# Out-projection weights of a hybrid attention block: the row sums and the gated halves moved to other steps

## The chip, the cores and the metric

One Trainium2 chip, one of its cores. The time is the device time of one execution in microseconds; a kernel's time is the median of its runs.

## The reference, cut to what matters

A block over 2048 latent tokens of width 1024, with 256 context tokens ahead of them. In float32:

```
mod   = silu(c) @ w_ada + b_ada                      # shift, scale, gate of 1024 each
h     = rmsnorm(x) * (1 + scale) + shift             # also for the context tokens
proj  = h @ w_in                                     # 1024 x 4096: q k v gate of two head groups
y     = [neighbourhood attention | retention] * silu(gates)
out   = rmsnorm(x + gate * (y @ w_out))
```

The change concerns `gate * (y @ w_out)`. `gate` is one number per output column, so the kernel multiplies the columns of `w_out` by it once, ahead of the projection, and stores the product. For that it needs `gate = silu(c) @ w_gate + b_gate`, where `w_gate` is the last third of `w_ada`.

## The kernel before, in words

The kernel is written in program order: each engine works through its own instructions in the order in which the Python code emits them, and nothing reorders them. TensorE computes all products in float32 halves (a rounded high part and the rest), three matmuls for each product. The order of the work around the change is this.

1. A first pass over the tokens, then a first stretch of values (`values`, with `u_v` and `tokform`, L374).
2. **The first pair of blocks** (`strassen(T, 0, 1, ...)`): the columns for q and the two gates, as a 2 x 2 product with seven multiplications (`w_set`, `prod`, L671). It runs over six sets of 256 columns (`SETS`). Each set has seven products of twelve 512-column matmuls, and four steps: after the 2nd, 4th, 6th and 7th product `step(n)` runs what is due. So a pair has 24 steps, 0 to 23; I number them so. `hooks` is a list of 24 lists of functions, one for each step. `w_sums` prepares the next set's weights one step at a time: casts on ScalarE (L624), subtractions on GpSimd (L625), sums on VectorE (L634 to L642).
3. **The second values** (the second call of `values`): ten units of 48 matmuls (L374), numbered 0 to 9. The stretch begins with the two context units, for which the normalised context is loaded again from DRAM (`cS`, L835). Beside it, `pump` drives the sums `h_sums` for the next pair, from blocks 2 and 3 that are loaded again (`hS`, L826).
4. **The second pair of blocks** (`strassen(T, 2, 3, ...)`), again 24 steps. Then attention, retention and the output.

The out-projection weights come in pieces of 128 x 512, two for each 128 rows, in a tile `wraw` with two buffers: sixteen pieces of `w_gate`, then sixteen of `w_out`.

- `wo_gate` (L744, VectorE) adds one piece of `w_gate`, times silu(c), to a running sum `gacc`. Sixteen calls, at steps 1 to 16 of the first pair.
- `wo_row` (L751 on TensorE, L752 on ScalarE) sums `gacc` over its partitions. One call, at step 19.
- `wo_mul` makes one gated half: it multiplies a piece of `w_out` by the row in place (L756, VectorE), casts it into a tile `g` (L758, ScalarE), subtracts (L759, GpSimd), and defers two stores to DRAM (`woS`, L761, on ScalarE's queue) and the next load of `wraw` (L739, on SyncE's queue). `g` has one buffer. Before, four calls lie beside the second values, after units 2, 4, 6 and 8, and twelve in the second pair, at its steps 0, 2, ... 22.

Stores and loads that are deferred wait in a list; `tick()` counts it down and issues what is due. It runs at the start of each step and at the end of each unit. At step 20 of the first pair `take(3)` issues four reloads of block 3; at step 21 `take_a` issues the two context loads and then four reloads of block 2. All of them are issued by SyncE, which works through its queue in order.

Of the kernel before, what the change touches and what calls it, by code (L numbers as in the profile page):

```python
# [82 lines left out]
def hybrid_kernel(ctx: ExitStack, tc: tile.TileContext, a: dict, out: bass.AP):  # L83
# [54 lines left out]
    def defer(n, fn):  # L138
        later.append([n, fn])

    def tick():
        for e in later:
            e[0] -= 1
        due = [e for e in later if e[0] <= 0]
        later[:] = [e for e in later if e[0] > 0]
        for e in due:
            e[1]()
# [190 lines left out]
    def w_parts(rw, lo=3, n=1):  # L338
        wh = wa.tile([P, KC, WG], F32R, name="whi")
        wl = wa.tile([P, KC, WG], F32R, name="wlo")  # L340

        def part(u, c):
            ks = slice(u * KH + c * KH // n, u * KH + (c + 1) * KH // n)
            h, l, r = wh[:, ks, :], wl[:, ks, :], rw[u][:, c * KH // n:(c + 1) * KH // n, :]
            nc.scalar.copy(h, r)
            eng = nc.gpsimd if lo >> u & 1 else nc.vector
            eng.tensor_tensor(l, r, f(h), ALU.subtract)  # L347

        return (wh, wl), [(lambda u=u, c=c: part(u, c)) for u in range(2) for c in range(n)]

    def w_split(rw, lo=3):
        w, parts = w_parts(rw, lo)
        for p in parts:
            p()
        return w
# [52 lines left out]
    def u_v(w, c0, tp):  # L408
        pm = yield from tokform(w, tp)
        vt = op.tile([P, 4, 4, 64], F32R, name="o")  # L410
        pv = pm.rearrange("p (g e d) -> p g e d", e=2, d=64)
        nc.scalar.copy(vt[:, :, ::3, :], pv)
        nc.vector.tensor_tensor(vt[:, :, 1:3, :], pv, f(vt)[:, :, ::3, :], ALU.subtract)
        s, o = (c0 - 1024) // WG, f(vt).rearrange("p (t h) e d -> p t (h e d)", t=2)
        if tp == 8:
            store(vS[s].rearrange("(t p) h d -> p t (h d)", p=P), o)
            return
        for e, j in enumerate(VORD):
            k0, cw = CWIN[j]
            dst = vB[s][:4 * cw, tp, e, :].rearrange("(t r c) d -> r c t d", t=2, r=2)  # L420
            for r in range(2):
                defer(1 + r, lambda dst=dst[r], src=o[64 * r + k0:64 * r + k0 + cw]: nc.sync.dma_start(dst, src))
# [62 lines left out]
    wcur = []  # L485
# [128 lines left out]
    def w_sums(rw):  # L614
        cut2 = lambda t: t.rearrange("p k w -> p (k w)").rearrange("p (s h k c) -> p s h k c", s=2, h=2, k=KH)
        a11, a21 = rw[0][:, :, 0:P], rw[0][:, :, P:WG]
        a12, a22 = rw[1][:, :, 0:P], rw[1][:, :, P:WG]
        W, tl = {}, {}

        def cut(key, n, s, r):  # L620
            if n not in tl:
                tl[n] = cut2(wa.tile([P, KC, WG], F32R, name=("whi", "wlo")[n % 2]))
            t = W[key] = tl[n][:, s]
            nc.scalar.copy(t[:, 0], r)  # L624
            nc.gpsimd.tensor_tensor(t[:, 1], r, f(t)[:, 0], ALU.subtract)  # L625

        V = nc.vector.tensor_tensor

        def p0():
            cut("a11", 0, 0, a11)  # L630
            cut("a12", 0, 1, a12)

        def p1():
            V(a11, a11, a21, ALU.subtract)  # L634
            V(a12, a12, a22, ALU.subtract)
            V(a12, a12, a11, ALU.add)
            V(a21, a21, a22, ALU.add)
            cut("a22", 1, 1, a22)

        def p2():  # L640
            cut("s4", 1, 0, a12)
            V(a22, a22, a11, ALU.subtract)  # L642

        def p3():
            cut("s3", 2, 1, a11)
            cut("s2", 2, 0, a22)

        def p4():
            cut("s1", 3, 0, a21)

        return W, [p0, p1, p2, p3, p4, None, load_w]
# [90 lines left out]
    def wo_gate(k, n):  # L742
        t, acc = wo["w"].pop(0), wo["acc"][:, n * 512:(n + 1) * 512]
        nc.vector.scalar_tensor_tensor(acc, t, silc[:, k, 0:1], acc, ALU.mult, ALU.add)  # L744
        defer(1, wo_next)
# [8 lines left out]
    def wo_mul(k, n):  # L754
        t, sl = wo["w"].pop(0), slice(n * 512, (n + 1) * 512)
        nc.vector.tensor_tensor(t, t, wo["acc"][:, sl], ALU.mult)  # L756
        w = wo["p"].tile([P, 2, 512], F32R, name="g")
        nc.scalar.copy(w[:, 0, :], t)  # L758
        nc.gpsimd.tensor_tensor(w[:, 1, :], t, f(w)[:, 0, :], ALU.subtract)  # L759
        for hl in range(2):  # L760
            defer(1, lambda hl=hl: nc.scalar.dma_start(woS[hl][k, :, sl], f(w)[:, hl, :]))  # L761
        defer(1, wo_next)
# [3 lines left out]
    def unit(g):  # L766
        for _ in g:
            pump["y"] += 1
            if pump["q"] and pump["y"] % pump["every"] == 0:
                pump["q"].pop(0)()  # L770
        tick()

    def strassen(T, A, B, W, mine, hook, last):
        for n, c0 in enumerate(SETS):
            if n + 1 < len(SETS):
                Wn, ahead = w_sums(wcur.pop(0))
            else:
                Wn, ahead = last, plain_next(last)
            w_set(c0, W, T, A, B, mine, ahead, hook)
            W, mine = Wn, ahead  # L780

    def values(vu, hook, at):
        for n, (w, c0, tp) in enumerate(vu):
            unit(u_v(w[0], c0, tp))
            if n == at:
                W, mine = w_sums(wcur.pop(0))
            if at <= n < at + 3:
                mine[n - at]()
            for fn in hook.get(n, ()):
                fn()  # L790
        while pump["q"]:
            pump["q"].pop(0)()
        mine[3]()
        return W, mine

    def vunits(order):
        return [(w, c0, tp) for w, c0, b in order for tp in (2 * b, 2 * b + 1) if tp < 9]
# [21 lines left out]
    w1 = w_split(wcur.pop(0), lo=0)  # L819
    load_w()  # L820
    spill_ctx(1)
    W, mine = values(vunits([([w0], 1024, 0), ([w0], 1024, 1), ([w1], 1280, 0), ([w1], 1280, 1)]), {0: [wo_open]}, 4)

    def take(b):
# [14 lines left out]
    hooks = [[] for n in range(24)]  # L839
    for k in range(8):  # L840
        for n in range(2):
            hooks[2 * k + n + 1].append(lambda k=k, n=n: wo_gate(k, n))
    hooks[19].append(wo_row)
    halves = [lambda k=k, n=n: wo_mul(k, n) for k in range(8) for n in range(2)]
    hooks[20].insert(0, lambda: take(3))
    hooks[21].insert(0, take_a)
    hooks[21].append(lambda: raws.pop(0)())
    mid = []
    strassen(T, 0, 1, W, mine, hooks, mid)
    w1 = []  # L850
    pump.update(y=0, every=4, q=raws)
    W, mine = values(vunits([(mid, 1024, 4), (mid, 1024, 3), (w1, 1280, 4), (w1, 1280, 3), (mid, 1024, 2), (w1, 1280, 2)]),
                     {0: [lambda: w1.append(w_split(wcur.pop(0), lo=0)), load_w, load_w], **{n: [halves.pop(0)] for n in (2, 4, 6, 8)}}, 6)
    T = T2
    hooks = [[] for n in range(24)]
    for n in range(12):
        hooks[2 * n].append(halves.pop(0))
    last = []
    strassen(T, 2, 3, W, mine, hooks, last)
# [762 lines left out]
```

## Time and profile before

| | |
|---|---|
| median of 3 runs | 1360.33 us (1356.68, 1360.33, 1361.18) |
| profiled execution, its own time | 1357.68 us |
| its span, first to last instruction | 1355.7 us |
| mean granted TensorE clock | 0.996 |
| TensorE busy | 1310.1 us, 97% of the span |

Times in the profile are microseconds from the start of the span. A row of the timeline is the start, the duration, the engine, the line, the operation, the tiles, the count, and in brackets how long the engine had been idle and what released it. SPq and ACTq are the instruction queues of SyncE and ScalarE, from which transfers are issued. In the order of the first pair, the last set (steps 20 to 23) runs from 332.8 to 352.7, and the second values from 352.7 to 411.5.

### The profile page before, as it was taken

How to read it: one execution, taken by the hardware profiler on the slowest of the kernel's cores; microseconds unless marked ns; L12 is line 12 of the kernel's file. 1: busy time of each engine (PE TensorE's matmuls, PEld its weight loads, DVE VectorE, ACT ScalarE, POOL GpSimd, SP SyncE). 2: the span in 40 equal slices, each digit the busy share in tenths (PEclk: the TensorE clock that was granted, in tenths of full speed). 3: DMA queues.
4: the chain of work that ended last, by engine and by line, in shares of the span. 5: the costliest groups of instructions: out<-in, count | busy, mean ns of one | idle time of the engine just before them, and what ended most of it. 6: DMA issues, size and time to landing. Idle time of an engine off the chain costs nothing.

```text
span 1355.7 us, 23094 instructions
## 1 busy us (share of the span) xinstructions
PE 1310.1 (97%) x8236; PEld 1146.9 (85%) x8236; DVE 828.3 (61%) x1444; ACT 606.5 (45%) x1259; POOL 579.9 (43%) x569
## 2 busy tenths in 40 slices
PE   6999999999999999999999999999999899999997
PEld 2477899887897788998999889889999789888886
DVE  5687366676766755377767777776654633445345
ACT  4454343343533344455555465556643244333432
POOL 4443101554034664445535474655523154544442
PEclk9999999999999999999999999999999999999999
DMA  9386788464867656978587886666528888555433
GB/s 363 135 279 231 259 313 215 164 210 147 326 182 230 216 203 213 265 210 211 148 225 207 226 224 206 195 181 193 163 90 291 278 290 279 159 163 171 163 121 129
DMA packets 172085, 287.25 MB, mean 212 GB/s; under 512 B 17345, under 2 KB 92225, under 8 KB 170690
## 3 DMA queue, kind: packets, MB, share of 16 engines
q1 hardware_dynamic: 139554, 228.35, 55.8%
q10 hardware_dynamic: 32416, 57.42, 11.8%
q8 instruction: 66, 1.08, 0.3%
q14 instruction: 49, 0.40, 0.1%
HBM read 194.48 MB, written 91.23 MB: 211 GB/s over the span
## 4 chain that ended last, share of the span: by engine, by line
PE 70%; DVE 9%; DMA 8%; POOL 4%; issue 4%; ACT 3%; SPq 1%; ACTq 0%; DVEq 0%; POOLq 0%
PE mm L374 17%; PE mm L671 12%; PE mm L1463 11%; PE mm L363 7%; PE sS L1025 4%; PE tr L1052 3%; PE po L1073 3%; PE mm L1187 2%; PE mm L311 2%; PE tr L1054 2%; PE po L1075 2%; DMA v<-rvS 1%; PE mm L1375 1%; POOL hlo L531 1%; PE mm L1374 1%
## 5 line engine op out<-in xcount | busy, mean ns | idle before, releaser
L374 PE MATMUL mm<-whi,hlo 128*128 128x256 f32 x832 | 228.6, 282 | 1.0 <-DMA hlo<-cS 1.0
L374 PE MATMUL mm<-whi,hhi 128*128 128x256 f32 x768 | 224.3, 292 | 0.0
L374 PE MATMUL mm<-wlo,hhi 128*128 128x256 f32 x768 | 216.8, 282 | 0.0
L1056 ACT CAST pt<-tr 128x640 fp32r<-128x640 f32 (+1 forms) x128 | 95.6, 747 | 160.4 <-PE tr L1054 157.8
L1062 DVE TENSOR_TENSOR pt<-tr,pt 128x640 fp32r<-128x640 f32 (+1 forms) x128 | 114.0, 890 | 78.4 <-ACT pt L1056 77.2
L374 PEld LDWEIGHTS mm<-whi,hlo 128*128 128x128 f32 x832 | 156.6, 191 | 1.4 <-DMA hlo<-cS 1.3
L1045 POOL TENSOR_SCALAR sp<-sp,stt 128x640 f32<-128x640 f32 (+2 forms) x128 | 103.1, 808 | 106.3 <-DVE stt L1044 75.7
L374 PEld LDWEIGHTS mm<-whi,hhi 128*128 128x128 f32 x768 | 146.3, 191 | 0.0
L374 PEld LDWEIGHTS mm<-wlo,hhi 128*128 128x128 f32 x768 | 146.1, 190 | 0.0
L1034 DVE CUSTOM_DVE_ANT_0 sp<-sS,nb 128x640 f32<-128x640 f32 (+2 forms) x128 | 105.6, 825 | 33.4 <-DMA nb<-in_rpb_t_dram 20.7
L1039 ACT ACTIVATE sp<-sp,stt 128x640 f32<-128x640 f32 (+2 forms) x128 | 107.4, 839 | 20.3 <-DVE stt L1034 19.1
L625 POOL TENSOR_TENSOR whi<-st,whi 128x512 fp32r<-128x512 f32 x48 | 62.8, 1330 | 107.7 <-ACT whi L624 107.7
L363 PE MATMUL mm<-hhi,whi 128*128 128x512 f32 x256 | 108.2, 423 | 0.0
L363 PE MATMUL mm<-hlo,whi 128*128 128x512 f32 x256 | 102.0, 399 | 6.0 <-DVE hlo L265 2.1
L1025 PE MATMUL sS<-k,q 128*128 128x256 f32 (+3 forms) x512 | 99.1, 315 | 5.1 <-DVE stt L1034 4.7
L363 PE MATMUL mm<-hhi,wlo 128*128 128x512 f32 x256 | 102.0, 398 | 0.3 <-DVE wlo L347 0.3
L671 PE MATMUL mm<-hhi,whi 128*128 128x512 f32 x336 | 98.1, 395 | 1.6 <-POOL whi L625 1.6
L1463 PE MATMUL mm<-wor,y 128*128 128x512 f32 x384 | 95.7, 398 | 1.1 <-DVE xt L1472 1.1
L1472 DVE TENSOR_TENSOR xt<-mm,xt 128x512 f32<-128x512 f32 x64 | 43.9, 687 | 82.6 <-PE mm L1463 82.5
L1025 PEld LDWEIGHTS sS<-k,q 128*128 128x128 f32 x512 | 82.8, 188 | 12.0 <-DVE stt L1034 8.2
L1463 PE MATMUL mm<-won,y 128*128 128x512 f32 x336 | 89.9, 406 | 0.0
L625 POOL TENSOR_TENSOR wlo<-st,wlo 128x512 fp32r<-128x512 f32 x36 | 53.1, 1476 | 75.8 <-ACT wlo L624 73.7
(258 smaller groups left out, 3051.5 us busy)
## 6 DMA issues: line engine op xcount, KB each, us to landing
st<-in_w_in_dram SPq DMA_DIRECT2D x64, 512.0 KB
q<-qS SPq DMA_DIRECT2D x64, 256.0 KB
hlo<-hS SPq DMA_DIRECT2D x20, 512.0 KB
k<-kS SPq DMA_DIRECT2D x16, 576.0 KB
kS<-o SPq DMA_DIRECT2D x16, 512.0 KB
vB<-o SPq DMA_DIRECT2D x64, 128.0 KB
qS<-o ACTq DMA_DIRECT2D x16, 512.0 KB
woS<-g ACTq DMA_DIRECT2D x32, 256.0 KB
```

What stands on the lines that cost most here:

```text
L363: nc.tensor.matmul(pm[:, :n], ww[:, k, cs], h[:, k, :], start=(k == 0 and i == 0), stop=(k == KC - 1 and i == 2))
L374: nc.tensor.matmul(pm[:, t * WG:(t + 1) * WG], h[:, k, o:o + P], ww[:, k, :], start=(k == 0 and i == 0), stop=(k == KC - 1 and i == 2))
L625: nc.gpsimd.tensor_tensor(t[:, 1], r, f(t)[:, 0], ALU.subtract)
L671: nc.tensor.matmul(pm, ww[:, k, :], hh[:, k, :], start=(k == 0 and i == 0), stop=(k == KH - 1 and i == 2))
L1025: nc.tensor.matmul(o, hd["q"][i][:, hl, j * P:(j + 1) * P], k, start=(hl == 0), stop=(hl == 1))
L1034: nc.vector.tensor_tensor_reduce(T["sp"][:, :n], T["s"], nbz[big][:, o:o + n], -1.0, 3e38, ALU.add, ALU.min, T["st"][:, 0:1])
L1039: nc.scalar.activation(sp[:, :n], sp[:, :n], AF.Exp, bias=st[:, 0:1], scale=-1.0, accum_out=st[:, 1:2])
L1045: nc.gpsimd.tensor_scalar(sp[:, :n], sp[:, :n], st[:, 2:3], 0.0, ALU.mult, ALU.add)
L1056: nc.scalar.copy(pt[:, :ng_ + 2, 0, :], tr[:, :ng_ + 2, :])
L1062: nc.vector.tensor_tensor(pt[:, :n, 1, :], tr[:, :n, :], f(pt)[:, :n, 0, :], ALU.subtract)
L1463: nc.tensor.matmul(pm, yy[:, k, :], ww[:, k, sl], start=(k == 0 and i == 0), stop=(k == 3 and i == 2))
L1472: nc.vector.tensor_tensor(xts[t][:, sl], pm, xts[t][:, sl], ALU.add)
```

## The change

The sixteen `wo_gate` calls move to steps 1 to 12 (four of these steps get two). `wo_row` moves from step 19 to step 14. Six gated halves run in the first pair, at steps 16, 17, 18, 19, 22 and 23; none is left beside the second values; ten stay in the second pair, at its steps 0, 2, ... 18, so that steps 20 and 22 have none. At the end of `values`, one `tick()` is added ahead of the last piece of the weight sums.

```diff
@@ values
         while pump["q"]:
             pump["q"].pop(0)()
+        tick()
         mine[3]()
@@ the first pair
     for k in range(8):
         for n in range(2):
-            hooks[2 * k + n + 1].append(lambda k=k, n=n: wo_gate(k, n))
-    hooks[19].append(wo_row)
+            hooks[1 + (2 * k + n) * 3 // 4].append(lambda k=k, n=n: wo_gate(k, n))
+    hooks[14].append(wo_row)
     halves = [lambda k=k, n=n: wo_mul(k, n) for k in range(8) for n in range(2)]
     hooks[20].insert(0, lambda: take(3))
     hooks[21].insert(0, take_a)
     hooks[21].append(lambda: raws.pop(0)())
+    for n in (16, 17, 18, 19, 22, 23):
+        hooks[n].append(halves.pop(0))
@@ the second values
-                     {0: [lambda: w1.append(w_split(wcur.pop(0), lo=0)), load_w, load_w], **{n: [halves.pop(0)] for n in (2, 4, 6, 8)}}, 6)
+                     {0: [lambda: w1.append(w_split(wcur.pop(0), lo=0)), load_w, load_w]}, 6)
@@ the second pair
-    for n in range(12):
+    for n in range(10):
         hooks[2 * n].append(halves.pop(0))
```

ScalarE's order from step 18 to step 20 of the first pair, before. The two L685 are the activations of set 4's last outputs, ggS are their stores, the `whi` casts belong to the next set's weights, and L699 takes the last set's first product:

```order
L624 CAST wlo<-st 128x512
L685 ACTIVATE o_2748<-o_2748 128x512
L685 ACTIVATE o<-o 128x512
L151 DMA ggS_81<-o_2748 128x512
L151 DMA ggS_82<-o 128x512
L624 CAST whi<-st 128x512 x2
L752 COPY gacc<-mm 128x512 x2
L699 COPY e<-mm 128x512
```

And of the changed kernel:

```order
L624 CAST wlo<-st 128x512
L758 CAST g<-wraw 128x512
L685 ACTIVATE o_2766<-o_2766 128x512
L685 ACTIVATE o<-o 128x512
L761 DMA woS_91<-g 128x512
L761 DMA woS_92<-g 128x512
L151 DMA ggS_81<-o_2766 128x512
L151 DMA ggS_82<-o 128x512
L624 CAST whi<-st 128x512 x2
L758 CAST g<-wraw 128x512
L699 COPY e<-mm 128x512
L761 DMA woS_91<-g 128x512
```

The row copies L752 have left this place; two casts of gated halves (steps 18 and 19) and the stores of the halves of steps 18 and 19 now stand among the activations.

SyncE's queue around the reloads of step 20, before. `st` are weight loads; in brackets stands what an issue waits for: an engine, or the completion of an earlier transfer (the DMAHW names are eight completion counters that the transfers of both queues take turns on):

```order
L739 DMA wraw<-in_w_out_dram 128x512 [waits DMAHW4_49,DVE_49]
L176 DMA st<-in_w_in_dram 128x1024 [waits DMAHW2_49,Pool_49]
L176 DMA st<-in_w_in_dram 128x1024 [waits DMAHW7_49,DMAHW3_49,Pool_49]
L826 DMA hlo<-hS_90 128x1024 [waits DMAHW7_49,PE_49]
L826 DMA hlo<-hS_90 128x1024 [waits DMAHW0_49]
L826 DMA hlo<-hS_90 128x1024 [waits DMAHW2_49]
L826 DMA hlo<-hS_90 128x1024 [waits DMAHW3_49]
L835 DMA hlo<-cS_93 128x2048 [waits DMAHW4_49,PE_49]
```

And of the changed kernel (the lines of `take` are L827 and L836 there):

```order
L176 DMA st<-in_w_in_dram 128x1024 [waits DMAHW6_49,DMAHW3_49]
L176 DMA st<-in_w_in_dram 128x1024 [waits DMAHW7_49]
L739 DMA wraw<-in_w_out_dram 128x512 [waits DMAHW3_49,Pool_49]
L739 DMA wraw<-in_w_out_dram 128x512 [waits DMAHW1_49,Pool_49]
L827 DMA hlo<-hS_90 128x1024 [waits DMAHW3_49,PE_49]
L827 DMA hlo<-hS_90 128x1024 [waits DMAHW4_49]
L827 DMA hlo<-hS_90 128x1024 [waits DMAHW6_49]
L827 DMA hlo<-hS_90 128x1024 [waits DMAHW7_49]
L836 DMA hlo<-cS_93 128x2048 [waits DMAHW0_49,PE_49]
```

Two loads of `wraw` that wait for GpSimd now stand directly ahead of the reloads of block 3; the second of them fills the buffer that the half of step 19 frees.

ScalarE's order beside the last units of the second values, before (L412 casts a unit's values, L624 prepares the second pair's first weights):

```order
L412 CAST o<-mm 128x4x2x64
L761 DMA woS_91<-g 128x512
L761 DMA woS_92<-g 128x512
L624 CAST wlo<-st 128x512
L412 CAST o<-mm 128x4x2x64
L624 CAST wlo<-st 128x512
L758 CAST g<-wraw 128x512
L412 CAST o<-mm 128x4x2x64
L761 DMA woS_91<-g 128x512
```

And of the changed kernel:

```order
L624 CAST whi<-st 128x512 x2
L412 CAST o<-mm 128x4x2x64
L624 CAST wlo<-st 128x512
L412 CAST o<-mm 128x4x2x64
L624 CAST wlo<-st 128x512
L412 CAST o<-mm 128x4x2x64
```

The casts and the stores of the gated halves are gone from this stretch, and so are the loads of `wraw` that stood between the stores of values on SyncE's queue.

## Rows read from the trace of the kernel before

**Rows 1.** The page, busy time, share and instructions of each engine.

```profile
PE 1310.1 (97%) x8236; PEld 1146.9 (85%) x8236; DVE 828.3 (61%) x1444; ACT 606.5 (45%) x1259; POOL 579.9 (43%) x569
```

**Rows 2.** TensorE's waits, 190 to 560: total, times, longest.

```profile
PE mm L671 <- POOL whi L625: 1.6, 3, 1.2
PE mm L374 <- DMA hlo<-cS: 1.0, 1, 1.0
PE mm L671 <- ACT wlo L624: 0.7, 1, 0.7
PE mm L671 <- POOL wlo L625: 0.6, 1, 0.6
```

**Rows 3.** Timeline of TensorE: the row sum, the context unit, the last value matmul.

```profile
331.51 1.88 PE L751 MATMUL mm<-gacc,one 128*128 128x512 f32 x4
332.83 0.79 PE L671 MATMUL mm<-hhi,whi 128*128 128x512 f32 x1
...
353.96 0.38 PE L374 MATMUL mm<-whi,hlo 128*128 128x256 f32 x1 [1.02 <-DMA hlo<-cS]
...
411.40 0.28 PE L374 MATMUL mm<-wlo,hhi 128*128 128x256 f32 x1
```

**Rows 4.** Timeline of SyncE's queue, the reloads of block 3 and the context.

```profile
338.68 1.75 SPq L826 DMA_DIRECT2D hlo<-hS  x4
344.43 0.80 SPq L835 DMA_DIRECT2D hlo<-cS  x2
```

**Rows 5.** Stretches: busy time by engine, PEclk, DMA share, GB/s.

```profile
325.00:338.00 13.00, 13.00 (x54) 9.93 (x53) 5.95 (x9) 5.65 (x10) 4.77 (x5) 1.00 0.21 78
...
340.00:354.00 14.00, 12.98 (x58) 10.24 (x56) 9.12 (x8) 6.43 (x7) 0.00 (x0) 1.00 1.00 364
```

**Rows 6.** Waits of SyncE's queue, 200 to 540.

```profile
SPq L739 <- POOL g L759: 71.6, 9, 11.7
...
SPq L826 <- PE mm L671: 18.1, 1, 18.1
...
SPq L739 <- DMA woS<-g: 11.9, 5, 4.7
```

**Rows 7.** Timeline of ScalarE, steps 18 and 19 of the first pair.

```profile
330.35 0.63 ACT L685 ACTIVATE o<-o 128x512 f32<-128x512 f32 x1 [6.40 <-DVE o L710]
...
332.44 1.23 ACT L685 ACTIVATE o<-o 128x512 f32<-128x512 f32 x2 [0.44 <-DVE o L716]
333.10 0.92 ACTq L151 DMA_DIRECT2D ggS<-o  x2
334.12 1.14 ACT L624 CAST whi<-st 128x512 fp32r<-128x512 f32 x2 [0.45 <-ACT o L685]
```

**Rows 8.** Timeline of GpSimd: weights at step 19, a gated half.

```profile
334.82 2.54 POOL L625 TENSOR_TENSOR whi<-st,whi 128x512 fp32r<-128x512 f32 x2 [1.47 <-ACT whi L624]
...
403.78 1.29 POOL L759 TENSOR_TENSOR g<-wraw,g 128x512 fp32r<-128x512 f32 x1
```

**Rows 9.** Timeline of ScalarE beside the second values.

```profile
395.04 0.81 ACTq L761 DMA_DIRECT2D woS<-g  x2
...
418.00 0.59 ACT L412 CAST o<-mm 128x512 fp32r<-128x512 f32 x1 [1.63 <-DMA vB<-o]
418.02 0.88 ACTq L761 DMA_DIRECT2D woS<-g  x2
```

**Rows 10.** Timeline of SyncE's queue beside the second values.

```profile
397.63 0.36 SPq L739 DMA_DIRECT2D wraw<-in_w_out_dram  x1
...
422.85 0.36 SPq L739 DMA_DIRECT2D wraw<-in_w_out_dram  x1
```

**Rows 11.** Stretches near the start, columns as in Rows 5.

```profile
72.00:76.00 4.00, 2.59 (x13) 1.84 (x11) 4.00 (x6) 3.36 (x6) 2.32 (x2) 1.00 0.57 202
76.00:80.00 4.00, 3.45 (x10) 2.76 (x11) 4.00 (x4) 3.09 (x4) 4.00 (x2) 0.66 0.96 256
...
100.00:104.00 4.00, 2.56 (x13) 1.86 (x13) 4.00 (x5) 0.86 (x3) 2.98 (x1) 1.00 0.27 111
```

## The prediction

> **What bounds the kernel now.** I read the page first. TensorE is busy for 97% of the span and no other engine comes near [rows 1], so an edit on the other engines shows only where it makes or ends a wait of TensorE. No matmul is added or removed. I therefore asked for TensorE's waits in the stretch that the change touches, from the middle of the first pair to the start of attention [rows 2]. There are four groups, 3.9 us together. That is the most that the change can win, 0.29% of the time. 1.0 us of it is the first context unit, which waits for the context reload and goes on at 353.96 [rows 3]. The other 2.9 us lie in the second pair, where TensorE waits for the weight casts and subtractions of the next set.
>
> Why those are late is seen in ScalarE's timeline: it casts the last unit of values at 418.00, after a wait for the stores of an earlier unit [rows 9], while TensorE issued that unit's last matmul at 411.40 [rows 3]. ScalarE enters the second pair 6.6 us behind. The stores are late because SyncE's queue, which issues them in order, stood still ahead of them: its loads of `wraw` wait for GpSimd's subtraction, 71.6 us in all, and for the stores of a gated half on ScalarE's queue, 11.9 us [rows 6].
>
> Then I looked at the place where the work goes. There the reloads are issued by SyncE as soon as TensorE lets go of the buffer: block 3 at 338.68, the context at 344.43 [rows 4]; that wait of SyncE for TensorE is the 18.1 us in its list [rows 6]. Ahead of it the transfer engines are nearly idle, share 0.21 from 325 to 338; from 340 to 354 they are full, share 1.00 at 364 GB/s [rows 5]. So the context lands when all the bytes ahead of it have been moved, and TensorE already waits 1.0 us for it.
>
> **The change part by part.**
>
> *Row sums in twelve slots, row sum at step 14.* The same sixteen VectorE operations, four matmuls and two copies, earlier. The four matmuls of `wo_row` take the 1.3 us from 331.51 to 332.83 [rows 3]; moved ahead they delay steps 15 to 19 by 1.3 us and leave step 20 where it was. Two steps lie between the last `wo_gate` and the row sum, where there were three; TensorE shows no wait for it. Cost 0; were that cover gone, TensorE would wait for the last piece, one VectorE operation, below 1 us.
>
> *No halves beside the second values.* Four multiplications, casts and subtractions, eight stores and four loads leave the stretch in which ScalarE falls behind. With no load of `wraw` in SyncE's queue the eight stores of a unit are issued one behind the other, and the next cast need not wait. The 6.6 us of delay should mostly go, and with it the 2.9 us of waits. Bounds: 0, if the sums for the next pair alone keep ScalarE behind, and -2.9. Halves still run in every second step of the second pair, so I keep 0.3 us: **-2.6 us**. Of the two halves that leave steps 20 and 22 there I expect nothing, since TensorE hardly waits there.
>
> *Four halves in four steps running.* This is where I expect the loss. `g` has one buffer, so the cast of a half waits until the stores of the half before have landed; these stores wait for GpSimd, and they stand in ScalarE's queue at the start of the next step. I follow ScalarE from the activation that follows set 4's sixth product, 330.35 before [rows 7], now 331.65. Its end, the two stores of step 17's half (0.81 us, [rows 9]), one ggS store and a weight cast bring it to 334.2. How long such stores take to land is bounded by two rows: issued until 395.85, and the load behind them goes at 397.63, 1.8 us; issued until 418.90 and followed at 422.85, 3.95 us [rows 9, 10]. The transfers are few at this place, so I take 1.8. Step 18's cast then runs at 334.9 and ends at 335.5; the two activations (1.23) end at 336.7, the stores of its half at 337.5, the two ggS stores (0.92) at 338.4, the two weight casts (1.14) at 339.5 [rows 7]. Step 19's cast ends at 340.1. GpSimd has two weight subtractions first (2.54, then 1.29 for the half, [rows 8]): from 339.0 to 341.5, and the half until 342.8.
>
> Now SyncE. Directly ahead of block 3's reloads stands the load of `wraw` that takes the buffer of step 19's half, so it waits until 342.8. The reloads follow at about 343.2 instead of 338.68, **4.5 us later**, and the context behind them. In addition 0.26 MB of this load or of the half's stores has to be moved in the full stretch, 0.7 us at 364 GB/s [rows 5]. TensorE then waits about 6.2 us at the context unit instead of 1.0: **+5.2 us**. Bounds: 0 for the order if ScalarE and GpSimd finish before 338.68, then only bytes remain (0.8 MB, 2.2 us); and 4.3 us more if the stores of steps 17 and 18 each take 3.95 us to land.
>
> The Trainium skill ("DMA: Bandwidth & Descriptors", on issuing engines that are not separate DMA queues) says that transfers of all issuing engines run on the same 16 DMA engines and interleave. If that did not hold, the stores on ScalarE's queue would cost the reloads nothing and the sum would be 0.7 us lower. The full share in [rows 5] agrees with the rule.
>
> *What an idle TensorE costs behind it.* From 72 to 76 TensorE was busy for 2.59 of 4 us, and in the 4 us that follow the granted clock is 0.66 on the mean, a part of it at the lower level of 1.2 GHz; from 100 to 104 it was busy for 2.56 of 4 us without such a fall [rows 11]. A wait of 6 us is longer than either, so I expect the fall: 4 us at 0.66 and some at less than 1 behind it lose about **+1.7 us**. Bounds 0 and, if it comes twice, 3.4. The Trainium skill ("TensorE: Matmul & The Clock Gate", why this matters) warns of idle gaps between matmul bursts, behind which the clock is back at the lower rate; by it the fall is certain, by the row at 100 it is not, and without it the sum is 1.7 lower.
>
> *Halves at steps 22 and 23.* Their loads and stores (0.5 and 1.0 MB) come behind the context reload. ScalarE waits for them ahead of the first unit's cast, but TensorE has six accumulators and a unit takes 5.8 us, so nothing shows; if the second context unit's weights came late too, 1 us.
>
> *The added tick.* It issues four stores of values ahead of two casts that stand on other engines. SyncE's order stays the same: 0.
>
> **Sum.** -2.6 + 5.2 + 1.7 = +4.3 us on the profiled execution's 1357.68, that is 1362.0. That execution lies 2.65 us below the median and 1.7 us below the mean of the three runs (1359.4). Carried over by the mean, the median of the changed kernel should be **1363.7 us**, 3.4 us or 0.25% over the median of before. About 0.3% (4.1 us) is what a measurement of this kernel tells from no change.
>
> **The rivals.**
>
> A, my forecast: the reload waits behind the load of `wraw`. Chance 0.60. Its own range is 1359.5 (no fall of the clock, one store time less) to 1366; the bound of 0.3% lies in its middle, so I give half of it to slower and a little more to the same.
>
> B, the reload is not held: VectorE's product of step 19 is ready soon after 334, and were ScalarE not held at `g`, GpSimd would be through at 338. Then only the bytes remain, +2.2 - 2.6 = -0.4: 1359.0. For it speaks that ScalarE idles between its rows at 330 to 334 [rows 7]; against it the single buffer of `g`. Chance 0.25, the same.
>
> C, slower: the chain of `g` runs at the upper store time. Then GpSimd ends step 19's weight subtractions not at 341.5 but at 345.8, and the fifth product of the last set, which starts when the fourth is done at about 344.4 [rows 4], waits for them, besides a reload that is 4.3 us later still: +8.6, 1368.0. It decides from a store time of about 3.2 us on. Chance 0.10.
>
> D, faster: the waits of the second pair go in full and the reload is no later, -2.9 or at most -3.9 if the context came in time too: 1356.5. That is inside the bound of 0.3%, so only a run to run shift on top would show it as faster. Chance 0.05.
>
> **How the numbers follow.** Slower: 0.32 of A and C, 0.42. Faster: D, 0.05. The same: 0.28 of A and B, 0.53. The range leaves out the lower part of D and the upper of C: 1357.5 to 1368.
>
> **What would show it.** Right: in TensorE's waits the one for hlo<-cS grows to 5 to 7 us; SyncE's first reload of block 3 is issued at 342 to 345 behind a load of `wraw`; ScalarE's waits name woS ahead of L758; the granted clock drops for a few us after 359; the waits of L671 for L624 and L625 in the second pair shrink below 0.6 us. Wrong: the reload still goes at 338.7, or the context wait stays below 3 us, or the second pair's waits stay at 2.9 us, which would mean that the sums for the next pair and not the halves hold ScalarE.

## Result, and the profile after

The changed kernel takes 1362.44 us (median of 20 runs), the kernel before 1358.45 us (20 runs) on the same chips: a ratio of 1.0029, 95% interval 1.0018 to 1.0039. That is 4.0 us more, where 3.4 had been forecast. The profiled execution took 1363.55 us, its span 1361.7, 6.0 us over the span of before; it lies 1.1 us above its median, and that of before 0.8 below.

TensorE's waits from 190 to 570 (total, times, longest), to be held against [rows 2]:

```profile
PE mm L374 <- DMA hlo<-cS: 8.1, 2, 6.2
PE mm L671 <- POOL whi L625: 1.3, 1, 1.3
```

The waits for L624 and L625 in the second pair are gone. The one for the context has grown from 1.0 to 8.1 us, and one for `whi` has come in a new place, the last set of the first pair. TensorE's timeline shows where, beside [rows 3]:

```profile
347.05 1.67 PE L671 MATMUL mm<-hhi,whi 128*128 128x512 f32 x6 [1.33 <-POOL whi L625]
...
361.48 0.55 PE L374 MATMUL mm<-whi,hlo 128*128 128x256 f32 x1 [6.20 <-DMA hlo<-cS]
363.94 0.58 PE L374 MATMUL mm<-whi,hlo 128*128 128x256 f32 x1 [1.91 <-DMA hlo<-cS]
```

SyncE's queue, beside [rows 4]:

```profile
332.93 0.88 SPq L176 DMA_DIRECT2D st<-in_w_in_dram  x2
342.40 6.20 SPq L739 DMA_DIRECT2D wraw<-in_w_out_dram  x2
348.70 2.16 SPq L827 DMA_DIRECT2D hlo<-hS  x4
350.96 1.48 SPq L836 DMA_DIRECT2D hlo<-cS  x2
```

The first row, two weight loads, is needed further down. The issue of two loads of `wraw` lasts until 348.6, and only then do the reloads go: at 348.70 instead of 338.68, 10.0 us later. TensorE has the last piece of the context at 363.94 instead of 353.96, again 10.0 us later. What holds the loads is read on ScalarE and GpSimd, beside [rows 7, 8]. ScalarE, the casts of the halves of steps 17, 18 and 19, and one pair of stores:

```profile
330.43 0.62 ACT L758 CAST g<-wraw 128x512 fp32r<-128x512 f32 x1 [2.51 <-DMA woS<-g]
...
332.61 0.81 ACTq L761 DMA_DIRECT2D woS<-g  x2
...
340.33 0.62 ACT L758 CAST g<-wraw 128x512 fp32r<-128x512 f32 x1 [5.69 <-DMA woS<-g]
...
346.14 0.62 ACT L758 CAST g<-wraw 128x512 fp32r<-128x512 f32 x1 [1.21 <-DMA woS<-g]
```

The stores of step 17's half are issued until 333.42 and the cast that waits for them starts at 340.33: 6.9 us. GpSimd follows the casts:

```profile
341.08 1.29 POOL L759 TENSOR_TENSOR g<-wraw,g 128x512 fp32r<-128x512 f32 x1 [5.07 <-ACT g L758]
...
344.49 2.51 POOL L625 TENSOR_TENSOR whi<-st,whi 128x512 fp32r<-128x512 f32 x2 [2.11 <-ACT whi L624]
346.95 1.30 POOL L759 TENSOR_TENSOR g<-wraw,g 128x512 fp32r<-128x512 f32 x1
```

The weight subtractions end at 347.0, which is TensorE's wait of 1.3 us, and step 19's half at 348.25, which frees the buffer for SyncE's load. The stretches behind the idle time, then the second values from the end of the first pair on and the second pair, with the columns of [rows 5]. Of after:

```profile
359.00:362.00 3.00, 0.52 (x1) 0.28 (x1) 3.00 (x4) 0.29 (x1) 0.00 (x0) 0.72 0.96 407
362.00:365.00 3.00, 1.09 (x6) 1.06 (x6) 2.90 (x4) 0.00 (x0) 0.00 (x0) 0.50 1.00 404
365.00:368.00 3.00, 3.00 (x19) 3.00 (x19) 2.97 (x6) 1.20 (x2) 0.00 (x0) 0.64 1.04 418
...
355.28:422.90 67.62, 59.51 (x481) 59.25 (x482) 47.59 (x49) 26.71 (x35) 6.49 (x5) 0.95 0.78 249
422.90:539.60 116.70, 116.70 (x507) 94.81 (x506) 75.16 (x88) 46.26 (x79) 67.11 (x49) 1.00 0.61 202
```

And of before:

```profile
352.70:411.50 58.80, 57.78 (x481) 57.54 (x480) 42.15 (x45) 23.55 (x31) 12.19 (x6) 1.00 0.75 234
...
411.50:532.70 121.20, 118.24 (x506) 94.34 (x505) 75.07 (x89) 47.90 (x82) 69.54 (x51) 1.00 0.65 215
```

The second values take 8.8 us more: 7.1 of waits and 1.7 us in which the same matmuls are busy longer (59.51 against 57.78), since behind the idle time the granted clock is 0.50 (the level of 1.2 GHz) from 362 to 365 and a part of the time at that level on both sides. The second pair takes 4.5 us less, 116.7 against 121.2.

### The profile page after: what moved, and what is told of

Same layout as the page of the kernel before. It is cut to its first block, busy times and chain, and to the rows that moved or that the text cites. A ratio compares the mean times of both kernels' runs of the same rounds, so it can differ in the third digit from the quotient of the medians.

```text
span 1361.7 us, 23105 instructions
## 1 busy us (share of the span) xinstructions
PE 1310.5 (96%) x8236; PEld 1148.8 (84%) x8236; DVE 835.2 (61%) x1444; ACT 606.5 (45%) x1259; POOL 577.6 (42%) x569
## 4 chain that ended last, share of the span: by engine, by line
PE 76%; DVE 6%; DMA 6%; POOL 4%; ACT 3%; issue 3%; SPq 0%; ACTq 0%; POOLq 0%; DVEq 0%
PE mm L374 20%; PE mm L671 15%; PE mm L1466 11%; PE mm L363 7%; PE sS L1028 5%; PE tr L1055 3%; PE po L1076 3%; PE mm L1190 2%; PE tr L1057 2%; PE mm L311 2%; PE po L1078 2%; DMA v<-rvS 1%; POOL hlo L531 1%; PE mm L1378 1%; PE mm L1377 1%
## 5 line engine op out<-in xcount | busy, mean ns | idle before, releaser
L625 POOL TENSOR_TENSOR whi<-st,whi 128x512 fp32r<-128x512 f32 x48 | 65.2, 1379 | 137.6 <-ACT whi L624 102.0
L1466 PEld LDWEIGHTS mm<-wor,y 128*128 128x128 f32 x384 | 69.9, 188 | 17.3 <-issue 3.4
```

Source lines behind the costliest of these rows:

```text
L1466: nc.tensor.matmul(pm, yy[:, k, :], ww[:, k, sl], start=(k == 0 and i == 0), stop=(k == 3 and i == 2))
```

## The experiments

All ten hang on the same two numbers: how long the first pair and the second values take together (from the first to the last of their matmuls), and how long the second pair takes. The table gives them from the profiled execution of each kernel, as differences of the starts of the first matmuls of the stages, with the time of SyncE's first reload of block 3 (not corrected for when the pair began), and the ratio to the kernel before with its interval.

| kernel | first pair + values | second pair | reload | ratio |
|---|---|---|---|---|
| before | 177.2 | 121.2 | 338.68 | |
| the change | 188.0 | 116.7 | 348.70 | 1.0029 (1.0018 to 1.0039) |
| no halves at 22, 23 | 186.1 | 116.7 | 346.30 | 1.0028 (1.0013 to 1.0042) |
| loads held | 183.7 | 116.7 | 338.60 | 0.9986 (0.9974 to 0.9998) |
| values' halves to the second pair | 176.6 | 122.8 | 339.25 | 1.0039 (1.0026 to 1.0053) |
| sums, row and tick alone | 176.7 | 123.5 | 339.21 | 0.9993 (0.9978 to 1.0008) |
| 16, 18, 22, 23 | 178.7 | 116.7 | 338.49 | 0.9965 (0.9952 to 0.9978) |
| 16, 17, 18, 22, 23 | 184.1 | 116.7 | 344.97 | 0.9992 (0.9978 to 1.0006) |
| 14, 16, 18, 22 | 176.8 | 116.7 | 338.51 | 0.9946 (0.9934 to 0.9958) |
| the same once more | 177.0 | 116.7 | 337.85 | 0.9940 (0.9923 to 0.9956) |
| 12, 14, 16, 18 | 183.7 | 116.7 | 345.90 | 1.0011 (0.9998 to 1.0024) |
| quarter stores | 187.1 | 116.7 | 347.96 | one execution: 1364.68 against 1360.70 us |

**Without the halves of steps 22 and 23.**

```diff
-    for n in (16, 17, 18, 19, 22, 23):
+    for n in (16, 17, 18, 19):
...
-    for n in range(10):
+    for n in range(12):
```

> The changed kernel without the halves of steps 22 and 23, which go back to steps 20 and 22 of the second pair. Theory (the load of wraw behind step 19's half holds SyncE's reloads): nothing of the loss goes. SyncE's first reload of block 3 at 347 to 350, TensorE's wait for hlo<-cS 7 to 8.5 us, 1.002 to 1.004 of the kernel before. Rival (bytes and queue places of the halves at 22 and 23, 1.5 MB around the reloads): the wait falls to 4 to 6 us, 1.000 to 1.002.

The reload went at 346.30, a little earlier than forecast, the context wait was 7.9 us, and the ratio is that of the change. So the two halves behind the reload are no part of the loss that the ratios can tell, and two more halves in the second pair, at steps 20 and 22, cost that pair nothing.

In the profile the first pair and the values are 1.9 us shorter than in the change. Up to step 21 the two programs are the same, and yet the chain ran otherwise there. ScalarE, and SyncE's weight loads:

```profile
332.27 0.87 ACTq L761 DMA_DIRECT2D woS<-g  x2
...
336.80 0.62 ACT L758 CAST g<-wraw 128x512 fp32r<-128x512 f32 x1 [2.48 <-DMA woS<-g]
```

```profile
333.19 0.90 SPq L176 DMA_DIRECT2D st<-in_w_in_dram  x2
```

Both stores of step 17's half were issued by 333.14, ahead of the weight loads, and step 18's cast went 3.7 us later, at 336.80. In the change the first weight load was issued at 332.93, ahead of the second store at 332.98, and the same cast went 6.9 us behind the stores. Here step 18's stores took 4.6 us, the wait of 1.3 us for `whi` did not come, and the reload, counted from the start of the pair, was 7.6 us late; in the change it was 9.4.

**The loads held back.** In addition, the loads behind the halves of steps 18 and 19 are issued only at step 22.

```diff
-        defer(1, wo_next)
+        defer(hold, wo_next)
...
+    for n in (16, 17, 18, 19):
+        hooks[n].append(lambda n=n, h=halves.pop(0): h(22 - n if n > 17 else 1))
```

> As the kernel without halves at 22 and 23, and the two loads of wraw behind the halves of steps 18 and 19 are issued at step 22, behind the reloads of block 3, the context and block 2. The halves, their casts and their stores stay. Theory (queue order): the first reload goes at 338 to 341, the context wait falls to 1 to 3 us, what is left is the wait of about 1.3 us for step 19's weight subtractions; 0.998 to 1.001 of the kernel before. Rival (bytes: four halves' stores and loads in the full stretch): the wait stays at 5 to 8 us, 1.002 to 1.004. Rival (the chain of the single buffer g itself): the wait for whi L625 in the last set stays or grows past 2 us.

SyncE's queue and TensorE:

```profile
338.60 2.90 SPq L827 DMA_DIRECT2D hlo<-hS  x4
344.35 8.46 SPq L836 DMA_DIRECT2D hlo<-cS  x2
```

```profile
351.18 0.74 PE L671 MATMUL mm<-hhi,wlo 128*128 128x512 f32 x2 [1.19 <-ACT wlo L624]
352.54 4.14 PE L671 MATMUL mm<-hhi,wlo 128*128 128x512 f32 x10 [0.61 <-POOL wlo L625]
...
358.90 0.39 PE L374 MATMUL mm<-whi,hlo 128*128 128x256 f32 x1 [2.11 <-DMA hlo<-cS]
```

The reload is back at its old time, the context wait falls from 7.9 to 2.1 us, and the ratio falls from 1.0028 to 0.9986, with intervals apart and all four halves still in place. So the order in SyncE's queue makes the reload late and makes a clear part of the loss. It is not all of it: in the profile the first pair and the values are only 2.4 us shorter than without the halves of steps 22 and 23, and 6.5 us are left over the kernel before. The rest is the chain itself: step 19's cast now starts at 348.07, while the reloads run, so the weight cast behind it is late for the last set (1.8 us, with a granted clock of 0.59 from 352 to 355), and the second half of the context load waits 7.8 us for a ggS store on the other queue, on which its issue has to wait as the two queues share their completion counters; the context comes at 358.90, 4.9 us later than before.

**Only the halves of the values moved**, in the kernel before, to steps 3, 9, 15 and 21 of the second pair.

```diff
-  {0: [...], **{n: [halves.pop(0)] for n in (2, 4, 6, 8)}}, 6)
+  {0: [...]}, 6)
...
-    for n in range(12):
-        hooks[2 * n].append(halves.pop(0))
+    for n in [n for n in range(24) if n % 2 == 0 or n in (3, 9, 15, 21)]:
+        hooks[n].append(halves.pop(0))
```

> The kernel before with one part of the change: no halves beside the second values; their four go to steps 3, 9, 15 and 21 of the second pair, so that all sixteen are there. Row sums, row and first pair as before. Theory: the second pair's waits of 2.9 us go, the context wait stays at 1.0 us; 0.997 to 0.999 of the kernel before. Rival (the second pair's waits went because two halves left that pair, or sixteen halves are too many in it): waits of 2 to 5 us stay, 0.9995 to 1.001.

My forecast was wrong, in a way that helps. The waits near the start of the second pair (436 to 446 in the trace of before) are gone, as the theory says. New ones come from 476 on, 4.2 us in the pair, most of them behind steps 9 and 10: where three halves now follow in neighbouring steps, the casts wait for stores again (2.4 and 3.2 us). The longest comes just behind the pair. ScalarE and TensorE behind steps 20 to 22:

```profile
536.34 0.81 ACTq L761 DMA_DIRECT2D woS<-g  x2
...
544.57 0.62 ACT L758 CAST g<-wraw 128x512 fp32r<-128x512 f32 x1 [7.66 <-DMA woS<-g]
...
549.99 0.58 ACT L449 COPY o<-mm 128x512 f32<-128x512 f32 x1
```

```profile
550.62 0.58 PE L374 MATMUL mm<-whi,hhi 128*128 128x256 f32 x1 [4.67 <-ACT o L449]
```

It is the same chain elsewhere: the cast waits 7.66 us for the stores of the half before, and TensorE pays 4.7 us for it.

**Row sums, row and tick alone**, in the kernel before.

```diff
-            hooks[2 * k + n + 1].append(lambda k=k, n=n: wo_gate(k, n))
-    hooks[19].append(wo_row)
+            hooks[1 + (2 * k + n) * 3 // 4].append(lambda k=k, n=n: wo_gate(k, n))
+    hooks[14].append(wo_row)
...
+        tick()
         mine[3]()
```

> The kernel before with the rest of the change that moves no half: row sums in twelve slots, the row at step 14, the added tick. Theory: no wait comes or goes, 0.9995 to 1.0005 of the kernel before. Rival (two sums in one step hold VectorE and so the next set's sums, or the tick delays the last weight piece): a wait of 1 us or more at L671, 1.0005 to 1.0015.

No change can be measured. In the profiled execution the second pair's waits are longer than before (123.5 us for the pair), so they differ from one execution or kernel to the next while halves run beside the values; in all nine kernels without them beside the values and without neighbours in the second pair, it takes 116.7.

**Halves apart: steps 16, 18, 22 and 23.**

```diff
-    for n in (16, 17, 18, 19, 22, 23):
+    for n in (16, 18, 22, 23):
...
-    for n in range(10):
+    for n in range(12):
```

> The changed kernel with four halves in the first pair, at steps 16, 18, 22 and 23, none beside the second values, twelve at the even steps of the second pair. No two halves ahead of the reload lie in neighbouring steps. Theory (the chain of the single buffer g makes the load of wraw late): step 18's cast does not wait for stores, SyncE's first reload goes at 338.5 to 340, the context wait is 0.5 to 1.5 us, no wait of over 0.7 us at the start of the second pair, 0.997 to 0.999 of the kernel before. Rival (the second pair's waits differ from run to run and were no gain): 0.9995 to 1.001. Rival (any half whose load stands ahead of the reload holds it): reload at 342 or later, context wait 4 us or more, 1.001 to 1.003.

SyncE's queue, and TensorE at the second context unit:

```profile
336.18 0.33 SPq L739 DMA_DIRECT2D wraw<-in_w_out_dram  x1
338.49 1.84 SPq L827 DMA_DIRECT2D hlo<-hS  x4
...
359.84 7.52 SPq L739 DMA_DIRECT2D wraw<-in_w_out_dram  x2
367.41 6.72 SPq L176 DMA_DIRECT2D st<-in_w_in_dram  x4
```

```profile
371.37 0.50 PE L374 MATMUL mm<-whi,hlo 128*128 128x256 f32 x2 [0.32 <-ACT whi L345]
372.69 0.39 PE L374 MATMUL mm<-wlo,hlo 128*128 128x256 f32 x1 [0.82 <-DVE wlo L347]
```

The load goes at 336.18 and the reload at its old time; the context wait is 0.9 us. Here the halves of 22 and 23 do show: SyncE stands at their loads for 7.5 us, ahead of weight loads, and TensorE waits 1.1 us for the second context unit's weights. In the change, where TensorE comes to that unit later, no such wait is listed.

**One neighbour more: 16, 17, 18, 22 and 23** (eleven halves in the second pair).

> As the kernel with halves at 16, 18, 22 and 23, and one more at step 17 (eleven in the second pair, at its steps 0 to 20): three in neighbouring steps ahead of the reload, not four. Theory (each neighbour adds a wait for stores to the chain): step 18's cast at 338 to 340.5, its subtraction until 342.5, the reload at 342 to 344, the context wait 3 to 6 us, 0.9995 to 1.002 of the kernel before. Rival (only the half of step 19, which stands beside the reload, does the harm): reload at 339, wait 1 us, 0.997 to 0.999.

ScalarE and SyncE's queue; the first pair of this execution began 2.8 us later than that of before:

```profile
342.48 0.62 ACT L758 CAST g<-wraw 128x512 fp32r<-128x512 f32 x1 [5.65 <-DMA woS<-g]
```

```profile
344.55 0.33 SPq L739 DMA_DIRECT2D wraw<-in_w_out_dram  x1
344.97 4.20 SPq L827 DMA_DIRECT2D hlo<-hS  x4
```

Counted from the start of the pair the reload is 3.5 us late, the context wait is 3.3 us, and the last set waits 1.3 us for weights. So one, three and four halves in a row give a reload 0, 3.5 and 9.4 us late on that count (7.6 in the other execution with four); the half of step 19 is not alone to blame.

**Every second step: 14, 16, 18 and 22**, the row at step 13.

```diff
-    hooks[14].append(wo_row)
+    hooks[13].append(wo_row)
...
-    for n in (16, 17, 18, 19, 22, 23):
+    for n in (14, 16, 18, 22):
...
-    for n in range(10):
+    for n in range(12):
```

> The row sum at step 13, four halves in the first pair at every second step, 14, 16 and 18, and at 22; none beside the second values, twelve at the even steps of the second pair. Theory: as with halves at 16, 18, 22 and 23, reload at 338.5 to 340, context wait 0.5 to 1.5 us, 0.997 to 0.999 of the kernel before. Rival (the stretch before step 20 has no room for a third half): a wait of 1 us or more at L671 before 350, 0.999 to 1.001.

SyncE's queue behind the reloads:

```profile
360.06 0.33 SPq L739 DMA_DIRECT2D wraw<-in_w_out_dram  x1
363.27 6.58 SPq L176 DMA_DIRECT2D st<-in_w_in_dram  x4
```

With one load instead of two the weight loads go 4.1 us earlier than with 16, 18, 22 and 23, and from the middle of the first pair to the end of the second no wait of over 0.25 us is left but 0.7 us for the context. This version beats both kernels, by more than I forecast. It was run a second time:

> The kernel with halves at 14, 16, 18 and 22 once more. If its 0.9946 comes from the second pair (4.5 us) and from falls of the clock that happened to be absent elsewhere, it lies at 0.995 to 0.997 now; if the whole 7 us belong to the order, at 0.994 to 0.9955.

The ratio stays at 0.994, so it belongs to this order. The stages of the table give 4.9 us of it in the first run's profile (0.4 and 4.5); the stretch behind the second pair is 1.2 us shorter there too (821.8 against 823.0), with none of its instructions changed. For that part I have no cause.

**Still earlier: 12, 14, 16 and 18**, sums in ten steps, the row at step 11.

> Row sums in ten steps, the row at step 11, halves at steps 12, 14, 16 and 18, none at 22 and 23, none beside the second values, twelve at the even steps of the second pair. Theory (second pair without waits, reload on time, nothing in the way of the second context unit's weights): the second pair takes 116.6 us, context wait 0.5 to 1 us; 0.994 to 0.997 of the kernel before, as with 14, 16, 18 and 22. Rival (two sums in most steps of the first sets hold VectorE): a wait of 1 us or more at L671 before 300, 0.997 to 0.999.

The second pair is as short as forecast, but my forecast missed another wait. TensorE, and the stretches around it:

```profile
295.01 1.12 PE L751 MATMUL mm<-gacc,one 128*128 128x512 f32 x2 [0.87 <-DVE gacc L744]
299.00 1.22 PE L751 MATMUL mm<-gacc,one 128*128 128x512 f32 x1 [2.86 <-DVE gacc L744]
```

```profile
293.00:299.00 6.00, 2.27 (x8) 0.87 (x6) 5.86 (x11) 1.25 (x2) 0.16 (x1) 0.99 0.53 125
299.00:303.00 4.00, 4.00 (x9) 2.54 (x10) 1.14 (x2) 1.81 (x4) 1.11 (x1) 0.59 0.89 304
```

The row sum stands in TensorE's order one step behind the last sums, VectorE is not through, and 3.7 us of waits and a fall of the clock use up the gain.

**Quarter stores.** The change, but the stores of the four halves of steps 16 to 19 write 128 of 512 columns. The other columns of these pieces are filled late in the second pair with numbers that have no meaning, so the kernel leaves out a part of the output projection.

```diff
+            cut = slice(n * 512, n * 512 + 128) if k < 2 else sl
-            defer(1, lambda hl=hl: nc.scalar.dma_start(woS[hl][k, :, sl], f(w)[:, hl, :]))
+            defer(1, lambda hl=hl, cut=cut: nc.scalar.dma_start(woS[hl][k, :, cut], ...))
...
+    hooks[21].append(lambda: [nc.sync.dma_start(...) ...])
```

> The changed kernel, but the stores of the halves of steps 16 to 19 write only a quarter of their columns; the other columns of woS are filled at step 21 of the second pair with numbers that have no meaning, so this part of the output projection is left out. Instructions, queues and their order in the first pair stay. Theory (the chain of g is as long as the stores take to land): with short stores ScalarE's waits for woS ahead of L758 shrink from 3.7, 6.9 and 3.4 us behind the issue to about 2 us each, the reload goes at 342 to 345 instead of 348.7, and TensorE's wait for hlo<-cS is 3 to 6 us instead of 8.1. Rival (the chain is set by ScalarE's and GpSimd's own work, the stores' time does not matter): reload at 347 to 349, wait 7 us or more. A few us may be added at the end of the second pair by the filling stores; that stretch is not read.

ScalarE, SyncE's queue, and two stretches:

```profile
333.04 0.83 ACTq L762 DMA_DIRECT2D woS<-g  x2
...
339.57 0.62 ACT L758 CAST g<-wraw 128x512 fp32r<-128x512 f32 x1 [4.52 <-DMA woS<-g]
```

```profile
347.96 2.12 SPq L828 DMA_DIRECT2D hlo<-hS  x4
```

```profile
334.00:336.00 2.00, 2.00 (x10) 1.65 (x9) 1.99 (x4) 0.62 (x1) 0.87 (x1) 1.00 0.99 233
336.00:338.00 2.00, 2.00 (x10) 1.64 (x10) 0.69 (x1) 0.00 (x0) 0.42 (x1) 1.00 0.99 267
```

My forecast was wrong here. Stores of a quarter of the bytes still land 5.7 us after their issue (333.87 to 339.57), against 6.9, and the reload is only 0.7 us earlier, 1.2 counted from the start of the pair. The stores' own size does not set the time; the transfer engines are full from 334 on whatever the stores hold, with two weight loads (`st`, 1 MB) that SyncE issued at the same moment, the first at 333.02.

What sets it, as far as the rows show, is whether these loads are issued ahead of the second store. They were in the change (332.93 against 332.98, 6.9 us), with 16, 17, 18, 22 and 23 (334.98 against 335.20, 6.8 us) and here (333.02 against 333.42, 5.7 us). They were not in the kernel with held loads (332.52 against 332.39, 4.8 us) and in the one without the halves of steps 22 and 23 (333.19 against 332.78, 3.7 us). Some tenths of a microsecond decide, although the order within each engine is the same in the five programs up to there. These are five executions as they fell; the loads were not moved or taken away on purpose. Nor was a second buffer of `g` tried, which might take away the cast's wait by itself.

## Why the prediction was right, and where its steps were not

The time was right to 1.3 us and the mechanism was the forecast one: the reload of block 3 behind a load of `wraw` that the chain of `g` holds. That this order makes the reload late is shown by the held loads, and that neighbouring halves make the chain by the kernels with 16 and 18 against 16, 17 and 18. Three sizes were off, and they cancelled in part: the first pair and the values lost 10.8 us where my terms gave 6.9, and the second pair gained 4.5 where I had 2.6. That the total came so close is in part luck.

- *The landing of the stores, 1.8 us with 3.95 as the bound: the step that failed.* I wrote "the transfers are few at this place". They are few up to 333; then the set's weight loads start, the first of them issued ahead of step 17's second store. Measured were 3.7, 6.9 and 3.4 us for steps 16, 17 and 18 (3.8, 3.7 and 4.6 without the halves of steps 22 and 23). Step 18's cast ran at 340.33, not 334.9; the reload went at 348.70, not 343.2.
- *The context's wait, +5.2.* It is +7.1. The 10.0 us by which the reload is late arrive in full at the context; TensorE itself comes to the unit 2.6 us later (355.28 against 352.7), so it does not wait for all of them.
- *Rival C.* Its condition, a store time from about 3.2 us on, was met, and its wait came: 1.3 us for step 19's weight subtractions, at the place given. It did not come in the kernel without the halves of steps 22 and 23, although its stores took 3.7 us and more, so 3.2 us as the point from which it comes is not borne out. The reload lies nearer to C's (4.3 us behind 343.2) than to my forecast; C's total of +8.6 did not come, since the gain was larger too.
- *The clock, +1.7.* Measured 1.73 us (59.51 less 57.78). Of the 9 us from 359 on with a clock of 0.72, 0.50 and 0.64, TensorE was busy for only 4.6, so much of the fall cost nothing.
- *The second pair, -2.6 with -2.9 as the bound.* The pair is 4.5 us shorter, in every kernel without halves beside the values and without neighbours in the second pair. The list of waits had 2.9; another 1.5 us stood in TensorE's busy column, 118.24 against 116.70, for the same matmuls. My bound from the list of waits was too tight.
- *Row sums, row at 14, tick: 0.* Right: 0.9993 with an interval that holds 1. That a missing cover would cost below 1 us was wrong; at step 11 the row sum waits 3.7 us.
- *Halves at 22 and 23: nothing, or 1 us if the second context unit's weights come late.* Both ends were seen: nothing in the change, 1.1 us with a punctual context.

With the measured sizes the sum is 10.8 for the first pair and the values (7.1, 1.3, 1.7, and 0.7 that no row names) less 4.5, +6.3 us over these stages. The first pair began 0.6 us later than before and the stretch behind the second pair was 0.9 us shorter, which makes +6.0 in the span. Against the medians it is 4.0, because the profiled execution of before lay 0.8 us below its median and that of after 1.1 above.

## What to carry to other kernels

A load that refills a buffer waits in its queue for whoever empties the buffer; what stands behind it in that queue inherits the wait, so look at what follows each such load before moving the work that empties it. Work through a single buffer that is stored from wants to be spaced by more than the landing time of its stores, and that time is read at the new place, beside the transfers that are issued just ahead of them there, not where the work stood before. And a list of waits is no bound on a gain: take the length of the stage from a version that has no waits.

## What the runs showed that I had not expected

The landing time did not follow the stores' size but what was issued ahead of them: 5.7 us for 64 KB each and 6.9 us for 256 KB each behind the first weight load, 3.7 us for 256 KB each ahead of it. The Trainium skill ("DMA: Bandwidth & Descriptors", on queues, rings and completion order) says that a transfer engine takes turns between the queues that have work, packet by packet. By that alone two stores of 64 KB beside loads on the other queue would be through early: an estimate from that page's fixed cost of about 2.0 us and half of the 233 GB/s of the row above is 3.1 us. The run gave 5.7, and the measurement decides. The same section of the Trainium skill says that the increment which reports a transfer lands only after every earlier write of its transfer engine, across its queues. The five executions above agree with that order.

The clock did not follow the busy time alone. From 72 to 80, ahead of all that changes here, TensorE is busy for 2.59 and then 3.45 us in the kernel before, and the granted clock falls to 0.66 in the second part [rows 11]. With halves at 14, 16, 18 and 22 it is busy for less in the first part and nothing falls:

```profile
72.00:76.00 4.00, 2.03 (x9) 1.40 (x9) 4.00 (x7) 3.37 (x6) 2.32 (x2) 1.00 0.90 276
76.00:80.00 4.00, 3.61 (x17) 2.68 (x16) 4.00 (x3) 1.86 (x2) 3.92 (x3) 1.00 0.98 328
```

The first pair begins at 234.3 and 234.2 us in the two kernels, so this is not the gain. With halves at 16, 18, 22 and 23 it is busy for 2.04 us in the first part, and the granted clock falls to 0.57 in the second. The same instructions of TensorE were followed by a fall in two kernels and by none in the third, and no run here tells why.
